# A planner that orders five engines: loads counted at 400 bytes a ns, and finer pieces of small tiles

## The chip, the cores and the metric

The kernel runs on one core of a Trainium2 chip. The core has a matmul engine (TensorE, PE in the profile; its weight loads are PEld), a vector engine (VectorE, DVE), a scalar engine (ScalarE, ACT), a general engine (GpSimd, POOL) and an engine that here only issues transfers (SyncE, SP). Each engine runs its own list of instructions strictly in order; semaphores make it wait for others. Sixteen DMA engines move data between memory (HBM) and on-chip memory (SBUF); matmul results land in eight PSUM banks.

The metric is the device time of one execution in microseconds (us), the median of several runs. A profile comes from one further execution and has a time of its own.

## What is computed

Two layers over 256 latent tokens and 256 context tokens of width 2048, in float32. Layer 0 runs neighbourhood attention (16 heads) and a bidirectional state-space scan (32 heads) side by side out of one input projection; layer 1 is a gated short convolution. Both are modulated by vectors that come from `c` and `c_ctx`.

```python
shift, scale, gate = adaln(c, ada_w[i], ada_b[i])          # silu(c) @ w + b, in three parts
h = modulate(rms_norm(x, norm_g[i]), shift, scale)         # the same for ctx in layer 0
# layer 0
p, pc = h @ w_in, hc @ w_in[:, COL_K:]
ya = neighbourhood_attention(q, k, v, kc, vc, rpb) * silu(gate_a)
yb = gated_group_rmsnorm(bidirectional_ssd(...) + d * xs, z, ssm_norm_g)
x = x + gate * (concatenate([ya, yb]) @ w_out)
# layer 1
bg, cg, hv, g = split(h @ sc_w_in, 4)
x = x + gate * ((silu(g) * bg * dw_conv(cg * hv, conv_w)) @ sc_w_out)
```

## The kernel before

**Weights.** Nearly all the work is products with weight matrices that are read once. A weight arrives in pieces of 128 x 1024 float32 (524,288 bytes, or half of that) in one of five `raw` buffers (nine during the start, when tiles that are not yet in use lend theirs; line 218). ScalarE casts a piece to a high part `wH` (line 458), VectorE subtracts to get the low part `wL` (line 465), and TensorE multiplies three times: high by high, low by high, high by low (lines 680 to 711). There are three buffers of each part (`NW`, line 205). The `raw` buffer is given back after line 465, and the next load is issued at once (line 428).

**The start.** Eight steps `j`. For each, TensorE multiplies eight pieces of the layer's gate weights (`ada`, line 763) with the conditioning vectors; the sums are turned (line 772) and added to the tables `ab0` and `g0` of the tile `small` (lines 776 to 782) to give scale `A0` and shift `S0`. In parallel the token rows (two tiles of 128 latent tokens, two of context) are loaded (line 618), squared and summed (lines 636 to 642), brought to their root by a power that reads `mhalf`, a part of the tile `const` (line 607), scaled (lines 648, 650), turned (line 660) and copied to `xm` (lines 663, 664). Then `hH` and `hL` (lines 798 to 804) are the modulated rows in two parts, and TensorE projects two of their sixteen blocks onto K, V, Q and part of B; lines 828 and 830 add the results up. `small` is loaded in two parts, columns 0 to 95 at the very start (line 395) and 96 to 435 later (line 565); `const` likewise, columns 0 to 161 (line 397) and 162 to 865 (line 566). The two later ones are put in behind the loads of the context rows.

**The later stages.** The other projections run one after another (lines 1548 to 1613), with the attention heads (`head_gen`) and the scan (`group_gen`, `make_x`) as side work; then `w_out`, the norm of layer 1, `sc_in` and `sc_out`. A background task (`gemv_gen`, lines 840 to 880) works off 128 further pieces of gate weights on VectorE (line 857) through the whole run.

**The planner.** No engine chooses its order at run time. While the program is written, the class `Plan` keeps a clock for each engine (`self.t`), the time at which each piece of each tile is written (`self.w`) and last read (`self.r`). Every instruction passes through `Plan.add`, which charges it by a table (`cost`) and moves the clocks; nothing of this reaches the chip but the order. A load on SP's queue is charged its bytes divided by `RATE`, one after another, with 1000 ns before and 1000 ns after (lines 115, 116). `Plan.keys` cuts a tile into pieces, by which writes and reads are told apart: 128 elements of a row in one piece, whatever the tile's width.

Work is split into tasks (Python generators), which say before each step what they wait for, for instance `W_("DVE", ps)`. After every few matmuls `pump` (line 326) asks `may` (line 296) which tasks may write their next step: for ScalarE and VectorE when the planned time of the inputs is at most 400 ns past the engine's clock, for TensorE when it is at most 100 ns past its own. `force` (line 347) writes the step with the earliest planned time until a condition holds. A weight is cast when its planned landing is at most 300 ns past the clocks (`splits_try`, line 491); a step of the background task is allowed 1000 ns later than its load. So the planned time of a load, and the pieces of the tiles, decide the order of each engine's list. The order of the loads themselves is fixed (lines 561 to 602); a load's place among SP's instructions follows the step that frees its buffer.

The semaphores on the chip do not come from `keys`: they follow the real overlap of the instructions' operands, and hold whatever the planner believed.

Of the kernel before, what the change touches and what calls it, by code (L numbers as in the profile page):

```python
# [37 lines left out]
class Plan:  # L38


    NAMES = {"PE": "PE", "DVE": "DVE", "Activation": "ACT", "Pool": "POOL", "SP": "SP"}
    RATE = 270.0

    def __init__(self):
        self.t = dict.fromkeys(("PE", "DVE", "ACT", "POOL", "SP"), 0.0)
# [4 lines left out]
    def keys(self, ap):  # L50
        a, n = ap.ap, ap.tensor.name
        if type(ap.tensor).__name__ == "Tile" and not n.startswith("dram"):
            lo = ap.offset % a[0][0] if a[0][0] else ap.offset
            hi = lo + sum(abs(s) * (c - 1) for s, c in a[1:])
            return [(n, u) for u in range(lo // 128, hi // 128 + 1)]
        if n.startswith("in_") or n.startswith("out_"):
            return []
        hi = ap.offset + sum(abs(s) * (c - 1) for s, c in a)
        return [(n, u) for u in range(ap.offset // 256, hi // 256 + 1)]
# [38 lines left out]
    def add(self, b):  # L98
# [10 lines left out]
        if op == "DMACopy":  # L109
# [4 lines left out]
            if e == "SP":  # L114
                self.dma = max(self.dma, s + 1000) + n / self.RATE
                done = free = self.dma + 1000
            else:
                done = free = max(self.dma, s + 1000) + n / self.RATE + 1500
            if any(a.tensor.name.startswith("dram") for a in ins + outs):
# [1884 lines left out]
```

## Time and profile before

| what | us |
|---|---|
| median of three runs | 1769.15 (1763.7, 1769.15, 1769.4) |
| the profiled execution, its own time | 1762.67 |
| its span, first to last instruction | 1760.9 |
| TensorE busy | 1728.3 |
| VectorE busy | 1292.8 |
| ScalarE busy | 785.3 |
| GpSimd busy | 191.0 |

The profile's page gives busy time by engine, the span in 40 slices, the DMA queues, a chain of waits followed back from the last instruction, and groups of instructions. Further views of the same trace list each engine's waits ("who waited for whom: total, times, longest"), the busy times in chosen stretches of the span, and the instructions in order of time ("start, duration, engine, line, operation, out<-in, idle time before it and what ended it"). A group of matmuls is shown as out<-moving,stationary or the other way round by its operands' names; `bank` is a PSUM bank. TensorE's clock was granted at 0.999 of full speed over the span.

The time line opens with the load issues from 0.74 us. TensorE's first matmul starts at 13.11 us, the first projection at 26.12 us; the eight steps of the start last to about 168 us, and the last output is written near 1757 us.

### The profile page before, as it was taken

How to read it: one execution, taken by the hardware profiler on the slowest of the kernel's cores; microseconds unless marked ns; L12 is line 12 of the kernel's file. 1: busy time of each engine (PE TensorE's matmuls, PEld its weight loads, DVE VectorE, ACT ScalarE, POOL GpSimd, SP SyncE). 2: the span in 40 equal slices, each digit the busy share in tenths (PEclk: the TensorE clock that was granted, in tenths of full speed). 3: DMA queues.
4: the chain of work that ended last, by engine and by line, in shares of the span. 5: the costliest groups of instructions: out<-in, count | busy, mean ns of one | idle time of the engine just before them, and what ended most of it. 6: DMA issues, size and time to landing. Idle time of an engine off the chain costs nothing.

```text
span 1760.9 us, 25272 instructions
## 1 busy us (share of the span) xinstructions
PE 1728.3 (98%) x9305; PEld 1442.4 (82%) x9305; DVE 1292.8 (73%) x2041; ACT 785.3 (45%) x1186; POOL 191.0 (11%) x300
## 2 busy tenths in 40 slices
PE   6999999999999999999999999999999999999998
PEld 4677988889888889888888898888878888888887
DVE  5566877888787987786888698876667776766555
ACT  5422335454354453353453444654435444444442
POOL 0000111013111012111012101110000000000000
PEclk9999999999999999999999999999999999999999
DMA  9987675577876677866577767787766888876774
GB/s 349 344 291 252 214 227 181 181 214 241 261 227 201 190 219 248 262 193 204 170 239 227 215 188 226 224 261 253 268 216 232 265 281 266 267 248 216 219 231 158
DMA packets 147629, 412.50 MB, mean 234 GB/s; under 512 B 34304, under 2 KB 48272, under 8 KB 147504
## 3 DMA queue, kind: packets, MB, share of 16 engines
q1 hardware_dynamic: 132112, 366.64, 64.0%
q0 software_dynamic: 15392, 44.24, 8.0%
q8 instruction: 73, 1.20, 0.3%
q14 instruction: 52, 0.43, 0.1%
HBM read 386.53 MB, written 25.59 MB: 234 GB/s over the span
## 4 chain that ended last, share of the span: by engine, by line
PE 94%; DVE 2%; DMA 1%; ACT 1%; issue 1%; SPq 0%; POOL 0%; DVEq 0%; ACTq 0%; POOLq 0%
PE bank L231 93%; PE bank L235 1%; DVE wL L465 1%; DMA raw<-in_ada_w 0%; ACT wH L458 0%; DMA half<-in_rows 0%; DVE hL L804 0%; SPq L618 0%; DMA raw<-in_sc_in 0%; DVE tmp L1283 0%; DVE h L1729 0%; DVE tmp L800 0%; ACT h L1748 0%; ACT hH L798 0%; DVE xm L664 0%
## 5 line engine op out<-in xcount | busy, mean ns | idle before, releaser
L458 ACT CAST wH<-raw 128x1024 fp32r<-128x1024 f32 (+1 forms) x440 | 459.5, 1045 | 664.0 <-PE bank L231 559.6
L465 DVE TENSOR_TENSOR wL<-raw,wH 128x1024 fp32r<-128x1024 f32 (+1 forms) x440 | 532.2, 1213 | 257.4 <-ACT wH L458 255.0
L231 PE MATMUL bank<-hH,wH 128*128 128x256 f32 (+1 forms) x1040 | 341.0, 328 | 0.9 <-ACT wH L458 0.9
L231 PE MATMUL bank<-hL,wH 128*128 128x256 f32 (+1 forms) x1040 | 337.0, 324 | 0.0
L231 PE MATMUL bank<-hH,wL 128*128 128x256 f32 (+1 forms) x1024 | 331.4, 324 | 3.1 <-DVE wL L465 3.1
L231 PE MATMUL bank<-wH,h 128*128 128x512 f32 x1024 | 316.8, 390 | 1.7 <-DVE h L1729 1.7
L231 PE MATMUL bank<-wH,hH 128*128 128x512 f32 x640 | 256.0, 400 | 4.8 <-ACT hH L798 2.6
L231 PE MATMUL bank<-wL,hH 128*128 128x512 f32 x640 | 249.9, 391 | 0.3 <-DVE wL L465 0.3
L231 PE MATMUL bank<-wH,hL 128*128 128x512 f32 x640 | 249.3, 390 | 0.1
L231 PEld LDWEIGHTS bank<-wH,h 128*128 128x128 f32 x1024 | 191.9, 188 | 43.5 <-DVE h L1729 3.0
L231 PEld LDWEIGHTS bank<-hH,wH 128*128 128x128 f32 x1040 | 197.8, 190 | 18.9 <-issue 2.0
L231 PEld LDWEIGHTS bank<-hL,wH 128*128 128x128 f32 x1040 | 197.8, 190 | 15.8
L231 PEld LDWEIGHTS bank<-hH,wL 128*128 128x128 f32 x1024 | 194.6, 190 | 19.4 <-DVE wL L465 4.1
L857 DVE SCALAR_TENSOR_TENSOR acc<-raw,csil,acc 128x512 f32<-128x512 f32 x240 | 179.1, 746 | 30.9 <-DMA raw<-in_ada_w 27.2
L231 PE MATMUL bank<-wL,h 128*128 128x512 f32 x512 | 199.4, 389 | 0.2 <-DVE wL L465 0.2
L231 PE MATMUL bank<-wH,mix 128*128 128x512 f32 x512 | 160.9, 391 | 0.0
L231 PEld LDWEIGHTS bank<-wH,hH 128*128 128x128 f32 x640 | 120.1, 188 | 36.3 <-issue 7.2
L231 PEld LDWEIGHTS bank<-wH,hL 128*128 128x128 f32 x640 | 120.1, 188 | 25.4 <-DVE hL L804 0.6
L231 PEld LDWEIGHTS bank<-wL,hH 128*128 128x128 f32 x640 | 120.1, 188 | 25.0 <-DVE wL L465 1.1
L231 PEld LDWEIGHTS bank<-wL,h 128*128 128x128 f32 x512 | 96.1, 188 | 20.6 <-DVE wL L465 0.6
L231 PEld LDWEIGHTS bank<-wH,mix 128*128 128x128 f32 x512 | 96.1, 188 | 20.4 <-issue 0.5
L231 PE MATMUL bank<-wL,mix 128*128 128x512 f32 x256 | 99.7, 390 | 0.0
(276 smaller groups left out, 1856.5 us busy)
## 6 DMA issues: line engine op xcount, KB each, us to landing
raw<-in_w_in SPq DMA_DIRECT2D x209, 512.0 KB
raw<-in_ada_w SPq DMA_DIRECT2D x163, 512.0 KB
raw<-in_sc_in SPq DMA_DIRECT2D x128, 512.0 KB
raw<-in_w_out SPq DMA_DIRECT2D x64, 512.0 KB
raw<-in_sc_out SPq DMA_DIRECT2D x32, 512.0 KB
dram_ptd<-tmp POOLq DMA_DIRECT2D x32, 256.0 KB, 4.9
D<-dram_ptd POOLq DMA_DIRECT2D x64, 128.0 KB, 5.6
tmp<-dram_csr SPq DMA_DIRECT2D x32, 256.0 KB
```

Of the source, the lines that this page charges most:

```text
L231: E(T.matmul(o, l, r, start=start, stop=stop, skip_group_check=True))
L235: E(T.transpose(o, i, ident if k == 128 else ident[:k, :k]))
L458: E(S.copy(H, v))
L465: E(V.tensor_tensor(out=Lo, in0=v, in1=H.bitcast(F32), op=ALU.subtract))
L857: E(V.scalar_tensor_tensor(out=acc, in0=v[:, j], scalar=csil[:, 2 * k + j:2 * k + j + 1], in1=acc, op0=ALU.mult, op1=ALU.add))
```

## The change

`RATE` goes from 270 to 400 bytes a ns. `keys` no longer uses 128 elements for every on-chip tile: a tile whose row stride is under 256 elements is cut into pieces of 4, a tile whose name begins with `small` or `const` (and is wider) into pieces of 2, and all others stay at 128. Tiles in DRAM keep pieces of 256.

```diff
-    RATE = 270.0
+    RATE = 400.0
...
             lo = ap.offset % a[0][0] if a[0][0] else ap.offset
             hi = lo + sum(abs(s) * (c - 1) for s, c in a[1:])
-            return [(n, u) for u in range(lo // 128, hi // 128 + 1)]
+            k = 4 if a[0][0] < 256 else 2 if n.startswith(("small", "const")) else 128
+            return [(n, u) for u in range(lo // k, hi // k + 1)]
```

The tiles under 256 elements a row are those of statistics and scales (`ssq`, `rx`, `A0`, `S0`, `statk`, `statq`, `s4`, `ss1`, `r1`, `A1`, `M1`), of the scan's decay (`dtl`, `csl`, `ncs`, `wst`, `wl`, `ebc`), the halved convolution weights (`cwh`, `cbh`, `scwh`) and the rows of the background task (`rowb`, `adab`).

## The prediction, made before the changed kernel was run

> **What bounds the kernel now.** I read the page's shares first, then the table of stretches, then every wait of TensorE, and last the order of time in the first 60 us, because that is where the loads and the parameter tables meet the planner.
>
> ```profile
> span 1760.9 us, 25272 instructions
> PE 1728.3 (98%) x9305; PEld 1442.4 (82%) x9305; DVE 1292.8 (73%) x2041; ACT 785.3 (45%) x1186; POOL 191.0 (11%) x300
> ```
> The change alters no instruction's work, only the order in which the planner writes instructions into each engine's queue. TensorE keeps its 9305 matmuls and so its 1728.3 us. The time can only move by what happens to the 1760.9 - 1728.3 = 32.6 us in which it is idle.
>
> The table of stretches says where those lie (columns: stretch, length, busy time and count of each engine, granted clock, DMA share, GB/s).
> ```profile
> 0.00:10.00 10.00, 0.00 (x0) 0.00 (x0) 2.90 (x12) 2.96 (x6) 0.89 (x6) 1.00 0.64 205
> 10.00:20.00 10.00, 6.77 (x48) 5.04 (x48) 5.76 (x16) 6.35 (x15) 0.64 (x2) 1.00 1.03 420
> 20.00:30.00 10.00, 7.79 (x69) 4.30 (x68) 6.05 (x16) 6.31 (x13) 0.00 (x0) 1.00 1.03 396
> 30.00:40.00 10.00, 8.56 (x36) 6.26 (x35) 6.65 (x21) 6.77 (x17) 1.59 (x4) 1.00 1.01 381
> ...
> 1400.00:1600.00 200.00, 200.00 (x900) 164.39 (x899) 140.13 (x166) 90.54 (x105) 19.17 (x33) 1.00 0.82 267
> ...
> 1700.00:1761.00 61.00, 55.31 (x245) 45.45 (x243) 34.47 (x40) 19.59 (x20) 0.00 (x0) 0.98 0.52 177
> ```
> The first 20 us hold 13.2 us of idle time, the last stretch 5.7 us, and a long stretch in the middle none at all. TensorE's own waits name the rest, first up to 200 us, then after it (columns: total, times, longest):
> ```profile
> PE bank L231 <- DVE rx L606: 13.1, 1, 13.1
> PE bank L231 <- ACT hH L798: 2.6, 2, 1.4
> PE bank L231 <- DVE sz L830: 1.5, 1, 1.5
> PE bank L235 <- ACT half L768: 1.0, 2, 0.5
> PE bank L231 <- ACT wH L458: 0.9, 1, 0.9
> PE bank L231 <- DVE gt L830: 0.8, 1, 0.8
> PE bank L231 <- DVE wL L465: 0.6, 2, 0.3
> PE bank L235 <- ACT xs L648: 0.3, 1, 0.3
> ```
> ```profile
> PE bank L231 <- DVE wL L465: 3.0, 3, 2.3
> PE bank L231 <- DVE h L1729: 1.7, 2, 1.4
> PE bank L235 <- DVE x1b L1643: 0.7, 1, 0.7
> PE bank L231 <- ACT Vt L1050: 0.6, 1, 0.6
> ```
> The 13.1 us are the first loads on their way, and the 5.7 us at the end are the last output's arithmetic and store: the planner can reorder neither. What another order could remove is 7.7 us before 200 us (2.6 + 1.5 + 1.0 + 0.9 + 0.8 + 0.6 + 0.3) and 6.0 us after it (3.0 + 1.7 + 0.7 + 0.6): **13.7 us, 0.8% of the span, is the most that this change can gain.** What it can lose has no such bound.
>
> A busy TensorE might hide waits inside its busy time, so I looked at the spacing of matmuls.
> ```profile
> 57.13 0.39 PE L231 MATMUL bank<-hL,wH 128*128 128x512 f32 x1
> 57.36 0.40 PE L231 MATMUL bank<-hH,wL 128*128 128x512 f32 x1
> 57.59 0.39 PE L231 MATMUL bank<-wH,hH 128*128 128x512 f32 x1
> ```
> Back to back they start 0.23 us apart; the 900 of 1400 to 1600 us take 200 / 900 = 0.222 us each. No wait is hidden there. The Trainium skill, page "Perfetto Trace Analysis", section "Identifying the Most-Contended Engine", holds matmul busy time a poor measure and weight-load busy time a better one; by that rule the 82% would leave 18% of the span open, and the spacing contradicts it here.
>
> **The change, part by part.** *RATE.* The planner lets a load of 524,288 bytes land after 1.94 us of transfer at 270 and 1.31 us at 400, 0.63 us apart, plus 1 us before and 1 us after. It casts, gates and multiplies in an order that follows those times. What the queues really move at the start, in slices of 1.5 us:
> ```profile
> GB/s 0 115 203 381 158 250 404 419 421 415 426 418 418 423 415 425 407 385 388 339 383 294 396 369 399 421 421 412 225 360 401 423 407 421 421 314 330 221 366 359
> ```
> Full queues move 415 to 426 GB/s, so 400 is nearer the truth than 270 in the stage where loads set the pace. The Trainium skill, page "DMA: Bandwidth & Descriptors", section "Specifications", gives a core about 358 GB/s from HBM, which speaks against 400; by it the estimate for the first 6.42 MB would be 17.9 us in place of 16.1 us, and the new planner would be early by 1.9 us. The slices above 415 disagree with it for this single core.
>
> *Keys.* The planner marks "when written" per piece of a tile. With pieces of 128 elements the second load of `small` (columns 96 on) shares a piece with `g0` and `ab0` (columns 32 to 95), and the second load of `const` (columns 162 on) one with `mhalf`. In the program both second loads stand ahead of line 780, which reads `g0`. So the old planner lets line 780 wait for them. By the code's sizes the bytes up to and with them are 49,152 + 82,944 + 2,097,152 (x) + 4,194,304 (first gate group) + 1,572,864 (K, V, Q) + 2,097,152 (context) + 174,080 = 10.27 MB: 38.0 us at 270, with the two allowances 40.0 us. With the new keys line 780 waits for the gate group alone, 6.42 MB: 25.8 us at 270, 18.1 us at 400. On the chip the tables were never waited for:
> ```profile
> 15.32 4.85 PE L235 MATMUL bank<-const,xs 128*128 128x128 f32 x32
> ...
> 20.10 1.07 PE L231 MATMUL bank<-raw,cpad 128*32 128x256 f32 x16
> ...
> 22.61 0.16 DVE L780 TENSOR_TENSOR A<-A,small 128x4 f32<-128x4 f32 x1
> ...
> 25.47 0.60 ACT L798 ACTIVATE hH<-xm,S,A 128x256 fp32r<-128x256 f32 x1 [0.55 <-DVE S L782]
> ...
> 26.12 0.73 PE L231 MATMUL bank<-wH,hH 128*128 128x512 f32 x2 [1.22 <-ACT hH L798]
> ...
> 27.66 0.33 SPq L565 DMA_DIRECT2D small<-in_small  x1
> ```
> Line 780 ran at 22.61, five microseconds before the second table's load was even issued. So the new planner's picture of the start (gate group at 18, first projection at 21) is close to the chip's order, and the old one's (40) was not. In the later stages the other small tiles are written and read by one engine in order, or once, and their finer pieces change nothing: I cost them at zero, with no cover needed, since the real semaphores do not come from these keys.
>
> What the order does with it, place by place, each as a share of the waits quoted:
>
> (a) Gate chain, 20 to 26 us. 32 transposes stood ahead of the second half of the first gate sum; then came two copies of 0.5 us wait each and 1.22 us for `hH`: 2.2 us idle in that stretch. With loads believed sooner the gate sums come between the transposes, and some of these cover the copies. Bounds: 0 and -2.2 us. The chain of copy, turn, sum and scale stays serial, so I take -0.8.
>
> (b) The context rows' first turn.
> ```profile
> 28.50 2.35 DVE L465 TENSOR_TENSOR wL<-raw,wH 128x1024 fp32r<-128x1024 f32 x2
> ...
> 30.77 0.68 DVE L638 CUSTOM_DVE_ANT_0 tmp<-xs 128x512 f32<-128x512 f32 x1
> ...
> 34.90 0.38 PE L235 MATMUL bank<-const,xs 128*128 128x128 f32 x2
> ...
> 36.63 0.50 PE L231 MATMUL bank<-wH,hH 128*128 128x512 f32 x1 [1.36 <-ACT hH L798]
> ```
> It came after all 36 matmuls of the latent rows, and TensorE then stood 1.36 us. The new planner has the context tile at (9.04 MB) 24.6 us, some 3 us after its first projection, its norm done near 28 by the planner's costs, and the 36 matmuls (0.23 us each, 8.3 us) until 30: the turn is written a few matmuls sooner. But the norm's squares on VectorE begin at 30.77 behind two low parts of weights, which stay where they are, so written too soon the turn would hold TensorE instead, as long as now. Bounds: +1.4 and -1.4; taken -0.9, since the planner knows of those low parts.
>
> (c) The first `B` weight and the adds of lines 830 (0.9 + 1.5 + 0.8 us): the cast is behind the use of three weight buffers, the adds behind whatever VectorE was given before. The same again at another place would cost as much as it now does: bounds +3.2 and -3.2; taken -0.8, for the start alone.
>
> (d) The steady stage, 200 to 1700 us.
> ```profile
> L458 ACT CAST wH<-raw 128x1024 fp32r<-128x1024 f32 (+1 forms) x440 | 459.5, 1045 | 664.0 <-PE bank L231 559.6
> ```
> ```profile
> ACT wH L458 <- PE bank L231: 573.1, 310, 5.8
> ...
> ACT wH L458 <- DMA raw<-in_w_in: 13.4, 6, 4.0
> ...
> DVE acc L857 <- DMA raw<-in_ada_w: 27.2, 14, 3.8
> ```
> 310 of 440 casts waited for TensorE to free a weight buffer, 6 for a load. Weights are there long before, whatever the planner believes: this cover hides the rate. Loads believed 0.63 us sooner do let VectorE be put onto line 857 sooner, and its 14 waits will be more. Three weights of 12 matmuls, 2.7 us each, lie ahead of TensorE, so a hold of VectorE shorter than about two of them, 5.4 us, costs nothing. Bounds +7 (priced below) and -6.0; taken 0.
>
> Sum: -0.8 - 0.9 - 0.8 + 0 = **-2.5 us** against the profiled execution, 1760.9 to 1758.4 of span, or 1762.67 to 1760.2 us of its own time. The three runs' median is 1769.15 (1763.7 to 1769.4); I carry the same difference there: **1766.6 us**, -0.14%. A measurement of this kernel can tell about 0.3%, 5.3 us, from no change, so this is no measurable change.
>
> **The rivals.** *Most of the waits go.* If the start follows the new plan closely and the reshuffle also clears the places after 200 us, 6 to 13.7 us vanish: about 1760 us from the median. For it: the old planner was wrong by 40 against 22.61 exactly at the start, where half of the removable waits lie. Against it: the chip's order at the start was already sensible, with TensorE idle only 3.65 us from 20 to 40 us by the stretches above, part of which the serial chain needs.
>
> *Slower: VectorE is held by loads that the planner believes landed.* It has happened once in this trace:
> ```profile
> DVE half L1203 <- DMA half<-in_rows: 6.1, 1, 6.1
> ```
> VectorE stood 6.1 us behind this one small load, and TensorE then waited 2.3 us for `wL`, the longest of that row. A load in a crowded queue lands later than 400 bytes a ns say. The point from which it decides is a hold of 4 to 5.4 us (3.8 cost nothing, 6.1 cost 2.3). Three more holds like this one give +7 us, about 1776 us. Against it: no gate load has yet held VectorE beyond that point.
>
> *The plan changes and the order hardly does.* Then the times agree within 1 us, 1769 us. Against it: the start's planned times move by some 20 us. By the skill's rule on weight loads more than 13.7 us could be won; the spacing leaves that 1 in 50, inside the first rival.
>
> **How the numbers follow.** Small gain or nothing that can be told: 0.50 for the forecast and 0.06 for an unchanged order; most of the waits go: 0.24; held VectorE: 0.20. So faster 0.24, same 0.56, slower 0.20. The range takes in both sides and the spread of the runs before (1762.67 profiled to 1769.4): low 1762.67 less 6.7 (half of 13.7), 1756; high 1769.4 plus 7, 1776.5.
>
> **What would show it.** TensorE keeps x9305 and 1728 us within 2. (a) `hH` starts before 25.47, the 32 transposes are broken up by gate matmuls. (b) The pair of turns comes before the last latent matmul, the 1.36 us shrinks. (d) The waits of casts and of line 857 for loads grow from 13.4 and 27.2 us, without TensorE's wait for `wL` rising above 3.0. I am wrong if `PE <- DVE wL` or a norm-stage row grows by 5 us, if the start is not shorter though the order is the planned one, or if the busy time itself changes.

## The result, and the profile after

The changed kernel is slower. Its median is 1822.12 us (six runs, 1815.03 to 1825.19) against 1768.52 us for the kernel before (six runs, 1763.7 to 1770.87): a ratio of 1.0302 with a 95% interval of 1.0278 to 1.0326, or +53.6 us. The profiled execution took 1815.03 us, the one before 1762.67.

The page of the changed kernel opens with these lines. The file has one line more ahead of the code shown here, so L458 of before is L459 now, L857 is L858, L1467 is L1468.

```profile
span 1813.3 us, 25257 instructions
PE 1748.2 (96%) x9305; PEld 1448.0 (80%) x9305; DVE 1292.4 (71%) x2041; ACT 784.6 (43%) x1186; POOL 189.6 (10%) x300
```

TensorE runs the same 9305 matmuls. Its idle time went from 32.6 to 1813.3 - 1748.2 = 65.1 us, and its busy time, which should not have moved, grew by 19.9 us.

The table of stretches says where. The first three rows are of before, the next three of after, cut at places with nearly the same number of matmuls (the x behind the first busy time).

```profile
0.00:200.00 200.00, 179.15 (x1180) 131.59 (x1181) 123.71 (x248) 75.31 (x136) 3.13 (x11) 1.00 0.81 292
200.00:1110.00 910.00, 907.16 (x5215) 782.61 (x5215) 727.51 (x1226) 409.34 (x664) 142.96 (x214) 1.00 0.70 218
1110.00:1761.00 651.00, 642.00 (x2913) 528.21 (x2911) 441.60 (x569) 300.62 (x387) 44.95 (x75) 1.00 0.73 239
```
```profile
0.00:200.00 200.00, 177.63 (x1166) 126.07 (x1167) 122.77 (x248) 74.68 (x135) 3.13 (x11) 1.00 0.79 290
200.00:1150.00 950.00, 921.84 (x5213) 789.44 (x5212) 736.87 (x1239) 409.97 (x667) 142.50 (x215) 0.99 0.68 212
1150.00:1814.00 664.00, 648.69 (x2930) 532.46 (x2928) 432.74 (x556) 300.00 (x385) 44.00 (x74) 1.00 0.71 230
```

The middle stretch, where the attention heads and the scan run beside the projections, holds 40 us of the loss. The start is some 3 us later (14 matmuls fewer by 200 us, 0.222 us each), the end some 9 (13 us, less 17 more matmuls). This middle is the steady stage that the prediction took at 0.

TensorE's waits in the changed kernel (total, times, longest):

```profile
PE bank L232 <- DVE wL L466: 17.6, 17, 2.4
PE bank L232 <- DVE rx L643: 12.7, 1, 12.7
PE bank L232 <- DVE tmp L1468: 7.1, 4, 2.2
PE bank L232 <- ACT qH L1120: 5.0, 2, 3.2
PE bank L232 <- DMA raw<-in_ada_w: 3.0, 8, 0.6
PE bank L232 <- DMA half<-in_strict: 2.1, 1, 2.1
PE bank L232 <- DVE qL L1123: 1.9, 2, 1.7
```

The wait for low parts of weights went from 3.6 (0.6 + 3.0) to 17.6 us. Four rows are new: the scan's decay (`tmp` L1468), the heads' operands (`qH`, `qL`) and the scan's mask (`strict`), together 16.1 us. So are waits of the start's gate matmuls for their own loads, 3.0 us, and three smaller rows of the same kind, 2.3 us together. The row of `rx` is the first loads on their way, as before.

What VectorE and ScalarE wait for, in the same kernel:

```profile
DVE acc L858 <- DMA raw<-in_ada_w: 97.0, 47, 5.8
```
```profile
ACT wH L459 <- PE bank L232: 544.2, 290, 6.5
...
ACT tmp L1450 <- DMA tmp<-dram_csr: 17.6, 14, 3.0
ACT wH L459 <- DMA raw<-in_w_in: 15.6, 6, 3.4
```

VectorE stood 97.0 us in front of gate weights that had not landed, 47 times; before it was 27.2 us in 14. The casts hardly moved: 290 (310 before) still wait for TensorE and 6 for `w_in`; the scan's decay rows cost ScalarE 17.6 us where they cost 7.4.

One such hold, the longest, followed through the time line of the changed kernel (start, duration, engine, line, operation, idle time before it and its releaser):

```profile
676.43 1.54 DVE L858 SCALAR_TENSOR_TENSOR acc<-raw,csil,acc 128x512 f32<-128x512 f32 x2 [5.84 <-DMA raw<-in_ada_w]
...
677.88 0.61 DVE L1465 SCALAR_TENSOR_TENSOR tmp<-tmp,dtl,tmp 128x128 f32<-128x128 f32 x2
678.52 0.42 DVE L1468 TENSOR_TENSOR tmp<-tmp 128x256 f32<-128x256 f32 x1
...
679.00 0.43 PE L232 MATMUL bank<-tmp,xtm 128*64 128x128 f32 x2 [1.60 <-DVE tmp L1468]
```

Read it downwards: VectorE stands 5.84 us for a gate load and adds for 1.54. Behind it in its list are steps of the scan's decay. TensorE, in whose list the scan's matmul already stands, is idle 1.60 us until they are done. VectorE is not the bottleneck, yet its hold ended as idle TensorE. Shorter holds reached TensorE as well, here 4.89 and 3.81 us, through a low part that VectorE made behind the adds:

```profile
1220.19 1.54 DVE L858 SCALAR_TENSOR_TENSOR acc<-raw,csil,acc 128x512 f32<-128x512 f32 x2 [4.89 <-DMA raw<-in_ada_w]
...
1222.92 0.50 PE L232 MATMUL bank<-wL,mix 128*128 128x512 f32 x1 [1.58 <-DVE wL L466]
...
1433.27 1.54 DVE L858 SCALAR_TENSOR_TENSOR acc<-raw,csil,acc 128x512 f32<-128x512 f32 x2 [3.81 <-DMA raw<-in_ada_w]
...
1436.00 0.50 PE L232 MATMUL bank<-wL,h 128*128 128x512 f32 x1 [0.83 <-DVE wL L466]
```

Not every wait has a gate load at its head. TensorE's longest wait after the start is 3.19 us for `qH` until 473.92, and 1.70 us for `qL` follow. VectorE stood for a gate load just before (2.10 us, until 470.05), but the profile's chain of waits does not go through that hold (start, length, what):

```profile
466.00 5.03 DMA kqD_K<-dram_kqd
...
471.50 0.76 DVE KT L251 x2
...
472.73 0.72 DVE acc L858
...
474.14 1.22 DVE wL L466
...
475.96 0.41 DVE qL L1123
```

The head's keys, on a round trip through DRAM, landed only at 471.03. VectorE turned them, and then had two more gate adds and a low part in front of `qL`. TensorE's waits after 200 us come to 36.7 us in the changed kernel and to 6.0 us before. Followed back one by one, by the rule of that chain, to the first transfer on the way, 10.1 us (12 waits) lead to gate loads, 14.3 us to round trips of heads, scan and bias (`kqD_K`, `D`, `bias`), 4.2 us to weights, 2.8 us to two other loads and 5.4 us to none. In before none leads to a gate load.

Then the clock. These stretches of the changed kernel are 3.41 us long (length, busy times of PE, PEld, DVE, ACT, POOL, and behind them the granted clock):

```profile
470.27:473.68 3.41, 0.46 (x3) 0.03 (x1) 3.34 (x6) 0.84 (x2) 0.00 (x0) 1.00 0.99 353
473.68:477.09 3.41, 1.47 (x3) 0.87 (x4) 2.68 (x4) 1.12 (x2) 0.00 (x0) 0.50 0.67 225
...
589.73:593.14 3.41, 1.03 (x8) 0.83 (x8) 3.36 (x5) 2.60 (x4) 0.00 (x0) 1.00 0.00 0
593.14:596.55 3.41, 3.41 (x18) 3.41 (x17) 3.38 (x5) 1.30 (x2) 0.00 (x0) 0.50 0.69 196
596.55:599.97 3.42, 3.42 (x31) 3.42 (x30) 3.38 (x5) 1.39 (x2) 0.00 (x0) 1.00 0.68 243
```

After a stretch in which TensorE was busy for 0.46 or 1.03 us, it is granted half its clock for the next. The two stretches of 593 and 596 us show what that costs: 18 matmuls at 0.50, 31 at 1.00. There are seven stretches at half clock between 473 and 1075 us; in before there is none until 1758. Busy time spent in them is 1.47 + 6 x 3.41 = 21.9 us, of which half, about 11 us by this estimate, is lost. That is 11 of the 19.9 us by which the busy time grew. Some 6 of the other 9 are the ends of the waits, again by an estimate: the profile books a matmul at 0.39 us while the next one starts 0.23 us after it, so a wait behind a matmul adds 0.16 us to the busy time, and TensorE's waits went from 18 to 55 (37 x 0.16). Where the last 3 are stays open.

### The profile page after: what moved, and what is told of

Same layout as the page of the kernel before. It is cut to its first block, busy times and chain, and to the rows that moved or that the text cites. A ratio compares the mean times of both kernels' runs of the same rounds, so it can differ in the third digit from the quotient of the medians.

```text
span 1813.3 us, 25257 instructions
## 1 busy us (share of the span) xinstructions
PE 1748.2 (96%) x9305; PEld 1448.0 (80%) x9305; DVE 1292.4 (71%) x2041; ACT 784.6 (43%) x1186; POOL 189.6 (10%) x300
## 4 chain that ended last, share of the span: by engine, by line
PE 62%; DMA 13%; DVE 10%; issue 3%; ACT 1%; POOL 1%; SPq 0%; DVEq 0%; ACTq 0%
PE bank L232 61%; DMA raw<-in_ada_w 8%; DVE wL L466 3%; DVE acc L858 3%; DMA kqD_K<-dram_kqd 1%; DMA bias<-dram_rpbs 1%; DMA raw<-in_w_in 1%; DVE tmp L1284 1%; ACT wH L459 1%; PE bank L236 1%; DMA D<-dram_ptd 1%; DMA tmp<-dram_mrow 0%; POOL kqD_K L246 0%; DVE KT L251 0%; DMA tmp<-in_x 0%
## 5 line engine op out<-in xcount | busy, mean ns | idle before, releaser
L459 ACT CAST wH<-raw 128x1024 fp32r<-128x1024 f32 x439 | 458.4, 1046 | 646.8 <-PE bank L232 535.9
L466 DVE TENSOR_TENSOR wL<-raw,wH 128x1024 fp32r<-128x1024 f32 x439 | 530.5, 1215 | 217.3 <-ACT wH L459 215.9
L858 DVE SCALAR_TENSOR_TENSOR acc<-raw,csil,acc 128x512 f32<-128x512 f32 x240 | 179.5, 748 | 100.9 <-DMA raw<-in_ada_w 97.0
```

The source lines that it names most:

```text
L459: E(S.copy(H, v))
L466: E(V.tensor_tensor(out=Lo, in0=v, in1=H.bitcast(F32), op=ALU.subtract))
L858: E(V.scalar_tensor_tensor(out=acc, in0=v[:, j], scalar=csil[:, 2 * k + j:2 * k + j + 1], in1=acc, op0=ALU.mult, op1=ALU.add))
```

## Experiments

All are built from the kernel before and use its line numbers; "the whole change" means rate and pieces together. Each was timed beside the kernel before on the same chip (its medians lay between 1767.5 and 1769.2 us). The theory: loads believed too early put VectorE and ScalarE in front of them, and what is queued behind comes late to TensorE. The rivals: the pieces do it; the background task alone does it; any reordering costs as much.

**Which part.** `e1_rate_only` takes the new rate alone, `e2_keys_only` the new pieces alone; `e5_tables_only` cuts only `small` and `const`, `e6_tiles_only` only the tiles under 256 elements.

```diff
# e1                                  # e2: keys as in the change, RATE = 270.0
-    RATE = 270.0
+    RATE = 400.0
# e5 (e6: k = 4 if a[0][0] < 256 else 128)
-            return [(n, u) for u in range(lo // 128, hi // 128 + 1)]
+            k = 2 if a[0][0] >= 256 and n.startswith(("small", "const")) else 128
+            return [(n, u) for u in range(lo // k, hi // k + 1)]
```

> RATE 400 with the old keys. Theory A (steps on loads that the planner believes landed hold VectorE, and through it TensorE; the rate makes them believed too early): slower than before by 2 to 3.5%, 1800 to 1830 us, VectorE's waits for gate loads on line 857 at 60 us or more against 27.2 before and 97.0 with the whole change. Theory B (the finer keys reorder everything and the rate is harmless): within 1% of before, the waits on line 857 under 45 us.

> The new keys with RATE 270. Theory A: within 0.6% of before, 1758 to 1778 us, waits on line 857 between 15 and 45 us. Theory B: 1800 us or more, with TensorE's wait for the low parts over 12 us.

> RATE 270, fine pieces for the parameter tables alone. The keys by themselves cost 1.15% (1786.5 us). If the start is what they spoil (half-clock stretch at 60 us in that run): 1776 to 1786 us, the stretch at half clock near 60 us again, the stages after 200 us with TensorE's waits for low parts under 6 us. If the small tiles do it: within 0.4% of before.

> RATE 270, fine pieces for the tiles under 256 elements a row alone; the first 900 rows of TensorE's order are those of before. If the start is what the keys spoil: within 0.4% of before, 1761 to 1775 us. If the small tiles reorder the later stages for the worse: 1776 to 1786 us, with new waits of TensorE for the scan's or the heads' VectorE steps (L1467, L1122) after 200 us and none before.

| kernel | median us | ratio to before, 95% interval |
|---|---|---|
| e1, rate | 1822.79 | 1.0304 (1.0284 to 1.0325) |
| e2, pieces | 1786.53 | 1.0115 (1.0096 to 1.0134) |
| e5, tables' pieces | 1777.71 | 1.0047 (1.0028 to 1.0065) |
| e6, small tiles' pieces | 1777.50 | 1.0045 (1.0029 to 1.0062) |

The rate alone gives the whole loss, 55 us. The pieces alone cost 19 us, yet add nothing on top of the rate (54 us together): the parts do not add up, which is what one expects if each makes an order of its own. e2 lies in neither of its two ranges. e5 and e6 each lie in the range that blamed its half, and e5 has the half clock again, from 59 to 66 us; but their 9 us each are hardly more than the controls below, and I read nothing into them.

**Which queue.** `RATE` stands in two places: `e7_sp_400` puts 400 into line 115 (loads issued by SP), `e8_pool_400` into line 118 (the others).

```diff
# e7
-                self.dma = max(self.dma, s + 1000) + n / self.RATE
+                self.dma = max(self.dma, s + 1000) + n / 400.0
# e8
-                done = free = max(self.dma, s + 1000) + n / self.RATE + 1500
+                done = free = max(self.dma, s + 1000) + n / 400.0 + 1500
```

> Old keys; 400 for the loads on SP's queue (weights, gate pieces, table rows), 270 for the transfers that GpSimd and ScalarE issue. If the weight and gate loads are the ones believed too early: 1805 to 1830 us, nearly the whole 55 us of the rate. If the round trips through DRAM that GpSimd issues are: under 1785 us.

> Old keys; 270 for SP's loads, 400 for the transfers of the other queues. If the weight and gate loads are to blame for the rate's cost: within 0.7% of before, 1756 to 1780 us. If the round trips are: 1800 us or more, with TensorE waiting for the heads' casts (L1119) for 5 us or more.

e7: 1817.48 us, 1.0267 (1.0235 to 1.0300). e8: 1772.75 us, 1.0021 (1.0005 to 1.0038). It is SP's queue, which carries the weights and the gate pieces.

**How far.** `e10_rate_330`, `e9_rate_200` and `e15_rate_265` change the number alone, with the old pieces. `e15` is a control: 265 differs from 270 by 0.04 us a load. `e16_act_110` is another, with no bearing on loads: ScalarE's results are planned 10 ns later.

```diff
-    RATE = 270.0
+    RATE = 330.0                      # e9: 200.0, e15: 265.0
...
# e16 (RATE stays 270.0)
-            return n * 0.85 + 150 + (200 if len(outs) > 1 else 0), 100
+            return n * 0.85 + 150 + (200 if len(outs) > 1 else 0), 110
```

> Old keys, RATE 330, so that a load of 512 KB is planned 0.35 us sooner than at 270, some half of the step to 400. Theory A: between, 1785 to 1805 us, gate waits of 45 to 75 us. Rival C with a threshold: as at 400, or as little as the other small disturbances (1773 to 1780).

> Old keys, RATE 200: loads believed 0.68 us later than before. Theory A (early belief costs, with the price growing with the earliness): VectorE's waits for gate loads below 27 us, time at or under before, 1750 to 1770 us. Rival C (the order of before is a lucky one, and any disturbance costs half a per cent to one per cent whatever its sign): 1775 us or more.

> A control: old keys, RATE 265, every load 0.04 us later in the plan. If any disturbance of the order costs 2 to 3% (rival C in full): 1800 us or more. If a neutral disturbance costs little and the size of the rate is what counts: 1763 to 1785 us.

> A second control that touches no load: ScalarE's results are planned 10 ns later. Rival C in full: 1800 us or more. Else 1763 to 1785 us; with e15 it gives the size of a neutral disturbance.

| rate | planned landing of a lone 512 KB load, us | median us | ratio, 95% interval | waits of L857 for gate loads, us (times) |
|---|---|---|---|---|
| 200 | 4.62 | 1818.75 | 1.0278 (1.0261 to 1.0295) | 29.9 (12) |
| 265 | 3.98 | 1775.17 | 1.0039 (1.0026 to 1.0052) | 49.1 (24) |
| 270 (before) | 3.94 | 1769.21 | 1 | 27.2 (14) |
| 330 | 3.59 | 1805.27 | 1.0200 (1.0174 to 1.0226) | 84.6 (39) |
| 400, old pieces (e1) | 3.31 | 1822.79 | 1.0304 (1.0284 to 1.0325) | 93.0 (45) |

The planned landing is 1 us, the transfer, 1 us. Upwards of 270 the time grows with the holds of VectorE (e10 lies just above its expected ranges). Their sum is no price, though: the control at 265, which believes the loads later than before, has 49.1 us of them and is 0.39% above before, and e13 below has 39.0 us and is 1.7% above. What a hold costs depends on what stands behind it. The two controls cost 0.24% and 0.39%: a new order by itself can cost that here. The rival "any reordering" is ruled out for the whole 3%. For about 1% it is not: all 18 variants are slower than before, and e2 (1.15%) and e12 below (0.86%) leave the rate and the allowances of the loads as they were.

Downwards the theory's range (1750 to 1770 us) was missed, and the time lies in the rival's (1775 us or more). The trace shows another mechanism. At 200 the holds are about as before (29.9 us), but e9's background task falls behind: its last step runs at 1766.3 us, in before at 1553.8. TensorE's waits in e9, and its time line at the norm of layer 1, which needs that task's vectors:

```profile
PE bank L231 <- DVE acc L857: 29.6, 2, 27.0
...
PE bank L235 <- DMA rowb<-dram_mrow: 5.6, 1, 5.6
```
```profile
1355.94 0.65 PE L231 MATMUL bank<-acc,const 128*32 128x128 f32 x8 [27.04 <-DVE acc L857]
...
1362.19 0.28 PE L235 MATMUL bank<-const,rowb 32*128 32x32 f32 x1 [5.59 <-DMA rowb<-dram_mrow]
```

TensorE stands 27.0 and 5.6 us there. So 270 lies between two slopes: loads believed too early hold VectorE, loads believed too late starve the background task.

**The true landing time.** In the changed kernel's table of DMA issues the last column is the median time from issue to landing:

```profile
raw<-in_w_in SPq DMA_DIRECT2D x210, 512.0 KB, 4.7
raw<-in_ada_w SPq DMA_DIRECT2D x164, 512.0 KB, 5.5
```

The plan at 400 says 3.31 us for a load that finds the queue empty; the medians include loads that stood behind others, so the two are not quite the same quantity. `e4_landing` adds 1.4 us to the whole change, which makes it 4.71; `e11_true_load` does the same with the old pieces.

```diff
-                done = free = self.dma + 1000
+                done = free = self.dma + 2400
```

> The whole change, and each load on SP's queue is given 2400 ns after its transfer in place of 1000, so that a lone load of 512 KB is planned at 4.7 us, which is the median from issue to landing in the changed kernel's table of DMA issues. Theory A in both forms: 1755 to 1775 us, waits on line 857 under 35 us. Theory B: about 1820 still.

> Old keys, RATE 400 and 2400 ns after the transfer in place of 1000: a lone load at 4.7 us against 3.9 before, a row of loads closer together than before. Theory A: within 0.5% of before, 1760 to 1777 us, gate waits under 45 us. If the closer spacing of loads in a row is itself what costs: 1785 us or more.

e4: 1783.88 us, 1.0095 (1.0077 to 1.0113), with line 857 waiting 42.5 us (25 times). e11: 1786.38 us, 1.0098 (1.0077 to 1.0119), 40.8 us (19). One allowance takes back 38 of the 54 us, with either kind of pieces: some two thirds of the loss go with the planned landing time, at the same rate. The remaining 16 to 17 us are more than the theory allowed. Both times lie above its ranges (1755 to 1775 and 1760 to 1777 us), e4's waits on line 857 too, and e11 lies in the range of its rival, that the closer spacing of loads in a row is itself what costs. No run tests that rival alone; e18 below keeps that spacing and comes within 0.39% of before.

**Who is put in front of the loads.** `e3_gate_margin` lets each step of the background task be written only when its load is planned to have landed 3000 ns ago in place of 1000 (line 307; 400 ns of slack as before). `e12_margin_270` does that to the kernel before. `e13_cast_gate` makes both this task and the casts 1400 ns later. `e14_rows_late` gives the later landing only to what is neither a weight nor a gate piece.

```diff
# e3 (whole change), e12 (before)
-        rdy = plan.ready(aps) + (1000 if late else 0)
+        rdy = plan.ready(aps) + 1000 * (len(task.cond[0]) - len(eng))
...
-                yield W_("DVE+", RAW["gem", n, k][1])
+                yield W_("DVE+++", RAW["gem", n, k][1])
# e13 (whole change): gate steps 2400 in place of 1000, and
-            if plan.ready([RAW[pos["split"]][1]]) > max(plan.t["PE"], plan.t["ACT"]) + 300:
+            if plan.ready([RAW[pos["split"]][1]]) > max(plan.t["PE"], plan.t["ACT"]) - 1100:
# e14 (whole change)
-                done = free = self.dma + 1000
+                done = free = self.dma + (1000 if outs[0].tensor.name.startswith(("raw", "PT", "xtm", "yi")) else 2400)
```

> The whole change, and the background task's step on a fresh gate load is written 3000 ns past the planned landing in place of 1000. If the gate loads are the ones that hold VectorE (theory A in its narrow form): waits on line 857 under 35 us, time back to 1765 to 1785 us. If all loads believed early are to blame (wide form: context, rows and head loads too): waits on line 857 fall, the time only to 1790 to 1810. Theory B: about 1820 still.

> The kernel before (old keys, 270) with the gate step's margin at 3000 ns in place of 1000. Theory A: gate waits from 27.2 to under 12 us, time 1758 to 1770 us, within 0.4% of before since those waits were covered. Rival C: 1773 us or more.

> The whole change; the casts of weights and the background steps are both written 1400 ns later against the planned landing than in the changed kernel, the steps on table rows (bias, decay rows) not. With all of SP's loads 1400 ns later (e4) it was 1784 us. If casts and background steps carry the rate's cost: 1778 to 1792 us. If the rows carry a good part: 1795 us or more.

> The whole change; only SP's loads that are no weights and no gate pieces (bias, decay rows, residual rows, tables) land 2400 ns after their transfer in place of 1000. If the weights and gate pieces carry the rate's cost: 1805 us or more. If the rows do: 1775 to 1795 us, ScalarE's wait for the decay rows under 8 us.

| kernel | median us | ratio, 95% interval | L857's waits, us (times) |
|---|---|---|---|
| e3, gate steps later | 1802.53 | 1.0202 (1.0183 to 1.0221) | 14.3 (6) |
| e13, gate steps and casts later | 1799.59 | 1.0170 (1.0144 to 1.0196) | 39.0 (21) |
| e14, other loads later | 1820.02 | 1.0286 (1.0257 to 1.0315) | 91.9 (48) |
| e12, before with gate steps later | 1784.16 | 1.0086 (1.0069 to 1.0102) | 20.8 (11) |

e3 was to tell whether the background task is the whole of it. It isn't: its holds fell below those of before, and only 20 of the 54 us came back, as the wide form of the theory expected. Waits of e3:

```profile
DVE acc L857 <- DMA raw<-in_ada_w: 14.3, 6, 4.8
...
ACT wH L458 <- DMA raw<-in_w_in: 32.8, 10, 5.5
```

ScalarE's casts stand 32.8 us in front of `w_in` (15.6 in the changed kernel, but 29.1 in e1, so this row does not show that e3's edit put them there). Followed back as above, none of TensorE's waits after 200 us in e3 leads to a gate load any more; 6.7 us lead to `kqD_K`, 6.6 to `D` and 4.0 to the scan's decay rows. Holding back two users (e13) gives 22 us, the small loads alone (e14) 2 us, and the landing time itself, which moves all of them, 38. The shares do not add up: e13 lies in the range that blamed the small loads, e14 in the one that cleared them, and I can't split the loss among them. e12 missed its range (1758 to 1770 us, waits under 12 us) and pays the price of lateness: `PE <- acc L857` is 8.2 us in one wait at the norm of layer 1, the place of e9's stall.

**TensorE's own margin.** A side step of TensorE (a head's, a scan's) is written 800 ns after its inputs are planned. `e17_pe_margin` makes that 2800 with the whole change, `e18_land_pe` adds e4's landing.

```diff
-            return rdy + (0 if isurg else 800) <= now + 100
+            return rdy + (0 if isurg else 2800) <= now + 100
```

> The whole change; TensorE's steps of the side tasks (heads and scan groups) are written only 2800 ns after the planned time of their inputs, in place of 800. If half of the lost time is TensorE standing in front of side steps that have no lookahead: TensorE's waits for the heads' and groups' steps (L1119, L1122, L1467, L1151, L1157, L1159; 15.5 us with the change) under 5 us, and 1790 to 1808 us. If only the low parts of weights count: 1812 us or more.

> The whole change with SP's loads landing 1400 ns later, as e4 (1784 us), and the margin of 2800 ns for TensorE's side steps. If both places are what is lost: 1760 to 1775 us, near or at the kernel before. If the margin only moves the loss: 1780 us or more.

e17: 1807.63 us, 1.0230 (1.0197 to 1.0263), inside the expected range. TensorE's waits in e17:

```profile
PE bank L231 <- DVE wL L465: 11.6, 10, 3.1
PE bank L231 <- DVE tmp L1467: 7.5, 5, 2.7
...
PE bank L231 <- ACT qH L1119: 1.0, 1, 1.0
```

The heads' waits fell (`qH` 5.0 to 1.0), the scan's decay didn't (7.1 to 7.5), so the six side rows of the expectation came to 9.7 us and not to under 5. VectorE still stood 103.0 us in front of gate loads: the margin leaves the holds as they were. e18: 1774.43 us, 1.0039 (1.0024 to 1.0053), inside its expected range and where the control e15 lies. Its page and TensorE's longest row after the first loads:

```profile
PE 1735.7 (98%) x9305; PEld 1447.1 (82%) x9305; DVE 1291.6 (73%) x2041; ACT 785.6 (44%) x1186; POOL 191.4 (11%) x300
```
```profile
PE bank L231 <- DVE wL L465: 5.1, 5, 2.0
```

With later planned landings and a wider margin on the matmuls that hang on VectorE and ScalarE, busy time is back from 1748.2 to 1735.7 us, and the loss is gone to within a control's distance, at a rate of 400 and with the new pieces. No version was faster than the kernel before.

## Why the prediction was wrong

**(a) right in the number, by luck.** `hH` came before 25.47 and the first projection before 26.12, in the changed kernel's time line:

```profile
16.93 3.71 PE L236 MATMUL bank<-const,xs 128*128 128x128 f32 x32
...
24.23 0.60 ACT L799 ACTIVATE hH<-xm,S,A 128x256 fp32r<-128x256 f32 x1 [0.55 <-DVE S L783]
...
24.89 0.75 PE L232 MATMUL bank<-wH,hH 128*128 128x512 f32 x2 [1.23 <-ACT hH L799]
...
33.03 0.38 PE L236 MATMUL bank<-const,xs 128*128 128x128 f32 x2
...
35.09 0.50 PE L232 MATMUL bank<-wH,hH 128*128 128x512 f32 x1 [0.29 <-ACT hH L799]
```

The gain at 24.89 is 1.2 us (0.8 forecast), but it did not come from covered waits. The 32 transposes were not broken up: they still stand in one row, with the second half of the gate sums behind them. TensorE's waits on the way are 2.05 us in place of 2.2 (0.16 and 0.17 for gate loads, 0.49, 1.23). The first matmul came 0.41 us sooner (12.70), and the same 32 transposes took 3.71 us in place of 4.85; why, the runs do not say.

**(b) right.** The context rows' turns moved before the last latent matmuls (33.03), and the 1.36 us shrank to 0.29.

**(c) wrong in sign, taken with what replaced it.** Its own rows fell from 3.2 to 1.0 us (a gain of 0.8 us was forecast), but gate matmuls of the start were now placed ahead of their loads: 3.0 us in 8 waits and 2.3 us in three smaller rows, where there were none. By 200 us the start's gain was gone and TensorE stood 3 us behind. The new rate is near the queues' full speed at the start, and still the planned landing was too soon.

**Pieces of the small tiles: costed at zero.** Alone (e6) they cost 0.45%, hardly more than a control, and with the tables' pieces (e2) 1.15%. "The real semaphores do not come from these keys" is true and beside the point: the planned times do, and with them the order of later work.

**(d) is the step that failed: taken 0, measured some 49 of the 52 us by which the span grew (40 in the middle, 9 after it).** It rested on two sentences. "This cover hides the rate" was read from 310 casts waiting for TensorE, and it is true of the casts: 290 of them still do. But loads have other users. Gate pieces, decay rows and heads' turns have no three buffers ahead of them; I had seen the 14 waits of line 857 and argued that more of them would be free. "A hold of VectorE shorter than about two of them, 5.4 us, costs nothing" is the second. It looked at TensorE's weights only. Behind a held VectorE also stand the operands of heads and scan, whose matmuls have 0.8 us of margin in TensorE's list and not 5.4: the hold of 5.84 us at 676 ended as 1.60 us of idle time there. And the weights were not safe either: holds of 4.89 and 3.81 us, both under 5.4, ended as waits of 1.58 and 0.83 us for `wL`, which ran late 17 times in all. Gate loads are not the whole of it: of the 36.7 us that TensorE waits after 200 us, 10.1 lead to them. (d) had no term for waits that lead to round trips through DRAM and to late weights, nor for busy time.

**The rival "held VectorE" had a part of the mechanism and not the size.** It went to +7 us: three holds like the one of 6.1 us. Its point of decision, 4 to 5.4 us, lay above nearly all of the holds that came (47, mean 97.0 / 47 = 2.1 us, longest 5.8), and one of 3.81 us did cost. The 10.1 us that lead to gate loads are near its term, but the loss was 54 us. I gave it 0.20.

**"TensorE keeps its 1728.3 us" failed too**, by 19.9 us: about 11 of them are half clock after stalls, which I had not looked for, since before shows none until its end. "What it can lose has no such bound" was the sentence to follow up. I bounded the gain by counting waits, and the loss by one wait that had happened.

## What to carry to other kernels

Where a planner orders in-order engines by planned landings, a rate nearer the full queue's is not a landing time nearer the truth: compare the planned time of a load with the measured median from issue to landing, and remember that too early costs a held engine and too late a starved background task. To price a hold, look at everything queued behind the held engine, above all at the user with the smallest margin, and not only at the one with the deepest buffers. When one change alters every planned time, time a change without meaning first: here it cost 0.2 to 0.4%, so a single result of that size says nothing about its edit.

## What the runs showed of the hardware

The half clock comes in stretches of 3.41 us or whole multiples (6.83 at 473.68, one unbroken 40.96 us at e9's stall), but for the last of a trace, in which the program ends, and their starts lie on one grid: from 473.68 to 593.14 it is 119.46 us, 35 times 3.413; from 593.14 to 681.89 it is 26 times. All seven follow a stretch of that grid in which TensorE was busy for at most 1.69 of 3.41 us. In before the least busy stretches of its grid (laid from 1758.49) between 18 and 1755 us were followed by full clock; the first row is the least of all, the next two split the 2.3 us wait for `wL` between them (stretch, length, busy times, clock):

```profile
85.96:89.37 3.41, 1.94 (x9) 1.31 (x8) 3.31 (x6) 0.75 (x2) 0.00 (x0) 1.00 0.88 357
...
239.56:242.97 3.41, 2.12 (x18) 1.92 (x16) 0.57 (x2) 0.74 (x1) 0.00 (x0) 1.00 0.43 165
242.97:246.38 3.41, 2.37 (x19) 2.37 (x20) 3.41 (x4) 1.19 (x4) 0.00 (x0) 1.00 0.37 118
```

The changed kernel has two more near the edge, one on each side of it:

```profile
1006.16:1009.57 3.41, 1.63 (x10) 1.35 (x10) 3.41 (x4) 1.90 (x3) 0.54 (x1) 1.00 0.65 177
...
1067.59:1071.01 3.42, 1.69 (x14) 1.49 (x14) 3.38 (x6) 2.60 (x4) 0.00 (x0) 1.00 0.15 32
```

The stretch at 1006 was followed by full clock, the one at 1067 by half: the edge lies near half a stretch and busy time does not mark it exactly. In e1 the spread is wider: after 1.49 us of work (1354.58 to 1357.99) the clock stayed full, after 2.11 us (518.31 to 521.72) it was halved. The Trainium skill, page "TensorE: Matmul & The Clock Gate", section "Part 1: The HAM clock gate (the "warmup" mystery)", has the same length, a free-running window of 3413 ns, and names at least one idle window as what halves the clock. The length and the free run agree with these rows. The idle window does not: stretches with 1.03 and 1.69 us of work in them were enough, and by these rows a stall of some 2 us may cost 1.7 us more (half of 3.41, an estimate) when it falls into one stretch, and nothing more when two share it. That last is read from the rows and was not tried by an experiment.
